# 32 more tokens by gather, score lists at a later rank, gathers from an earlier stage, stored products by fours

## The chip, the cores and the metric

The kernel runs on one core of a Trainium2 chip. The metric is the device time of one execution in microseconds (us). Engines are called TensorE (PE in the rows; PEld is its weight load), VectorE (DVE), ScalarE (ACT), GpSimd (POOL) and SyncE (SP, which here only issues transfers).

## The reference

Two transformer blocks on 512 tokens of width 1024. The part that the change touches is the expert layer of the first block (PEER): 16,384 experts, each a row of `u` and a row of `v`; each token picks, for each of 8 heads, 16 experts by product keys.

```
q = (t @ wq).reshape(128, 8, 2, 128)
s = einsum('tpcd,pckd->tpck', q, sub_keys)
s1, i1 = top_k(s[:, :, 0], 16);  s2, i2 = top_k(s[:, :, 1], 16)
cand = s1[..., :, None] + s2[..., None, :]          # 256 sums
top, pos = top_k(cand, 16);  idx = i1*128 + i2 at pos
g = softmax(top)
a = gelu(einsum('tpkd,td->tpk', u[idx], t))
y = einsum('tpk,tpkd->td', g * a, v[idx])
x = x + gt2 * y
```

## The kernel before

Tokens are in four blocks of 128. For blocks 0 to 2 (`ND = NDENSE = 3`, `nd = 384` tokens) the layer is computed densely: for each of 128 groups `e` of 128 experts, all products with all tokens, times a matrix of gates that is zero for experts not picked. Block 3 is computed by gathers: `gather` (L834) fetches with an indirect transfer from GpSimd, for each of 128 picks, one row of `u` and `v` a token (1 MB), takes the dot product with `h2` (L840), gelu, gate, and adds the weighted `v` row to `pacc` (L846), in pairs of two picks; `run_gather` issues pairs up to a count. The sum of both ways is in f32: each dense product is three fp32r matmuls of a high and a low part (`split`: the cast `wh` on ScalarE, L190, and the difference `wl` on VectorE, L191; `mm` at L176 issues every matmul).

Stages, with their times in the profiled execution:

- 547 to 680 us, query stage (L799 to 812): for j = 0..7 a projection of `h2` by two weight tiles of `wq` (48 matmuls of 512 columns), then scores against the keys into `rsc`, kept for all j. At odd j `gemv_T` (L248) computes one modulation vector: eight weight tiles `wg` (own buffers, two), four small matmuls each, a copy of the row (`row`), eight `pick` matmuls that turn it into a column, and one add into `modT`.
- 680 to 905, U stretch (`s_part`, L681): for each expert group e, 24 matmuls `pS` of 384 columns, gelu into `S`; the first `PRE = 52` groups are stored to HBM (`sd`). VectorE works beside it through `routing` of blocks 3, 2, 1, 0: the lists of the 16 best per score vector (`top16`, five operations), the candidates, and the one-hot comparisons that read out the picks.
- 905 to 1165, one-hot stage: twelve groups of 32 tokens. For each, three more `s_part`, and four batches of 8 tokens: comparisons `Rh` and `Lq` on VectorE, `Lq` times gate (three batches by 8 ScalarE operations each, the fourth by one VectorE pass), 64 `pG` matmuls that make the gate matrix, stored to HBM as `gd`; one pair of gathers.
- 1165 to 1840, V stretch: for each of 128 steps, gate block `Gt` and product block `Sr` (from HBM, or `S` fresh from `s_part` for the 40 groups from `NSP = 88` on) give `W`; `W` is split, and 18 matmuls `po` of 512 columns add it times `v`. The other 104 gathers run beside it.
- From 1840 on: block by block `x`, loaded back from `x1d` (L961), plus the gated sum, a norm chain (`xsq`, `ss`, `rr`, `xs`), eight transposes and a split give the second block's input; then that block's projections start.

All weight tiles pass through a ring of four (`wr`) with rings for `wh` and `wl`. A scheduler orders each engine's instructions by a priority that follows the order in the program, moved by `issue_after`; a pool's buffer comes free when its last reader is done.

Of the kernel before, what the change touches and what calls it, by code (L numbers as in the profile page):

```python
# [10 lines left out]
F32 = mybir.dt.float32  # L11
# [113 lines left out]
NS = 10  # L125
NSP = 88
PRE = 52
GEN = 3
GR = 1
LAST = 4  # L130
# [5 lines left out]
def program(tc, a, out, tap=None):  # L136
# [37 lines left out]

    def mm(ps, lhs, rhs, first=True, last=True):
        PE.matmul(ps, lhs, rhs, start=first, stop=last)  # L176
# [438 lines left out]
    nd = ND * P  # L615
# [8 lines left out]
    gd = dp.tile([32, P, ND * 4, P], F32, name="gd")  # L624
    sd = dp.tile([NSP, P, ND * P], F32, name="sd")
    mp = pool(eM, "mid")
    gt2T = modT[:, 5, :]
    h2g = {b: mp.tile([P, D], F32, name=f"h2_{b}") for b in range(ND, NB)}
    idx = {b: mp.tile([P, P], I32, name=f"idx{b}") for b in range(ND, NB)}
    gate = {b: mp.tile([P, P], F32, name=f"gate{b}") for b in range(ND, NB)}  # L630
# [3 lines left out]
    def h2_of(b, x):  # L634
        t = h2g[b] if b in h2g else st.tile([P, D], F32, name="h2t")
# [62 lines left out]
    for e in range(EARLY):  # L698
        DMA.dma_start(sd[e], s_part(e, V.tensor_tensor))
# [15 lines left out]
    def top16(src, w, val, pos):  # L715
        t = r2.tile([P, P], F32, name="mr", bufs=2)[:, :w]
# [8 lines left out]
    def routing(b, sc):  # L725
        sv = r2.tile([P, 16, 16], F32, name="sv", bufs=2)
        si = r2.tile([P, 16, 16], U32, name="si", bufs=2)
        for j in range(16):
            top16(sc[:, j, :], P, sv[:, j, :], si[:, j, :])
# [39 lines left out]
        for s_ in range(2):  # L769
            eq = r2.tile([P, 8, 16, 16], BF16, name="eq", bufs=2)  # L770
# [496 lines left out]
```

## Time and profile before

| | |
|---|---|
| median of 3 runs | 2345.69 us (2344.76 to 2349.6) |
| profiled execution | 2337.86 us, its span 2336.1 |
| TensorE busy | 2259.9 us (97%) |
| VectorE busy | 1598.4 us (68%) |
| ScalarE busy | 980.3 us (42%) |
| GpSimd busy | 249.1 us (11%) |
| moved by DMA | 481.74 MB, mean 206 GB/s |

Busy time is the union of an engine's instructions; matmuls are pipelined, so the distance between two starts, not the length of one, tells what a matmul costs. The granted clock is the share of full speed that TensorE had. The largest groups on TensorE are the three kinds of `pS` (1024 each) and the three kinds of `po` (768 each).

### The profile page before, as it was taken

How to read it: one execution, taken by the hardware profiler on the slowest of the kernel's cores; microseconds unless marked ns; L12 is line 12 of the kernel's file. 1: busy time of each engine (PE TensorE's matmuls, PEld its weight loads, DVE VectorE, ACT ScalarE, POOL GpSimd, SP SyncE). 2: the span in 40 equal slices, each digit the busy share in tenths (PEclk: the TensorE clock that was granted, in tenths of full speed). 3: DMA queues.
4: the chain of work that ended last, by engine and by line, in shares of the span. 5: the costliest groups of instructions: out<-in, count | busy, mean ns of one | idle time of the engine just before them, and what ended most of it. 6: DMA issues, size and time to landing. Idle time of an engine off the chain costs nothing. (4 is left out here: it accounts for less than half of the span.)

```text
span 2336.1 us, 34601 instructions
## 1 busy us (share of the span) xinstructions
PE 2259.9 (97%) x13097; PEld 1942.3 (83%) x13097; DVE 1598.4 (68%) x3193; ACT 980.3 (42%) x1828; POOL 249.1 (11%) x159
## 2 busy tenths in 40 slices
PE   7999999998999999999999999999999999989998
PEld 4899986597779999999988888888888786666888
DVE  3674723354359977999689888888898627767344
ACT  4432333333234335877534333333333434446421
POOL 0000000000000000322222222222130000000000
PEclk9999999999999999999999999999999999999999
DMA  7111135625555574999999999999997231120221
GB/s 265 55 57 55 52 118 178 212 101 178 165 196 158 163 258 153 328 320 319 333 360 396 406 347 349 354 362 363 360 380 263 88 103 42 50 86 28 98 92 55
DMA packets 170871, 481.74 MB, mean 206 GB/s; under 512 B 14864, under 2 KB 87952, under 8 KB 153168
## 3 DMA queue, kind: packets, MB, share of 16 engines
q1 hardware_dynamic: 152272, 345.31, 42.7%
q0 software_dynamic: 18432, 134.23, 14.7%
q8 instruction: 103, 1.69, 0.3%
q14 instruction: 64, 0.52, 0.1%
HBM read 431.76 MB, written 46.66 MB: 205 GB/s over the span
## 5 line engine op out<-in xcount | busy, mean ns | idle before, releaser
L191 DVE TENSOR_TENSOR wl<-wr,wh 128x1024 fp32r<-128x1024 f32 (+1 forms) x378 | 456.7, 1211 | 362.3 <-ACT wh L190 359.8
L190 ACT CAST wh<-wr 128x1024 fp32r<-128x1024 f32 (+1 forms) x378 | 394.0, 1043 | 440.4 <-PE pm L176 196.1
L176 PE MATMUL pS<-h2h,wh 128*128 128x384 f32 x1024 | 348.2, 340 | 7.3 <-ACT S L695 7.2
L176 PE MATMUL pS<-h2h,wl 128*128 128x384 f32 x1024 | 346.1, 338 | 0.0
L176 PE MATMUL pS<-h2l,wh 128*128 128x384 f32 x1024 | 345.5, 337 | 0.0
L839 POOL DMA_INDIRECT uv<-in_uv_dram,idx x128 | 225.8, 1764 | 1006.9 <-DVE pacc L846 688.8
L176 PE MATMUL po<-wl,Wh 128*128 128x512 f32 x768 | 299.6, 390 | 1.8 <-DVE wl L191 1.8
L176 PE MATMUL po<-wh,Wl 128*128 128x512 f32 x768 | 299.5, 390 | 0.0
L176 PE MATMUL po<-wh,Wh 128*128 128x512 f32 x768 | 298.9, 389 | 0.0
L176 PEld LDWEIGHTS pS<-h2h,wh 128*128 128x128 f32 x1024 | 193.4, 189 | 11.7 <-ACT S L695 8.7
L176 PEld LDWEIGHTS pS<-h2l,wh 128*128 128x128 f32 x1024 | 193.3, 189 | 2.0 <-issue 0.8
L176 PEld LDWEIGHTS pS<-h2h,wl 128*128 128x128 f32 x1024 | 193.2, 189 | 0.0
L190 ACT CAST Wh<-W 128x384 fp32r<-128x384 f32 x128 | 65.7, 513 | 267.8 <-PE po L176 162.1
L176 PE MATMUL pm<-h2h,wh 128*128 128x512 f32 x432 | 173.5, 402 | 0.2 <-ACT cr L1106 0.2
L176 PE MATMUL pm<-h2h,wl 128*128 128x512 f32 x432 | 171.8, 398 | 0.0
L176 PE MATMUL pm<-h2l,wh 128*128 128x512 f32 x432 | 171.8, 398 | 0.0
L176 PEld LDWEIGHTS po<-wl,Wh 128*128 128x128 f32 x768 | 144.1, 188 | 31.9 <-DVE wl L191 2.6
L176 PEld LDWEIGHTS po<-wh,Wl 128*128 128x128 f32 x768 | 144.1, 188 | 30.3 <-DVE Wl L191 0.3
L176 PEld LDWEIGHTS po<-wh,Wh 128*128 128x128 f32 x768 | 144.2, 188 | 29.2
L846 DVE SCALAR_TENSOR_TENSOR pacc<-uv,dts,pacc 128x1024 f32<-128x1024 f32 x128 | 163.9, 1281 | 1.9
L840 DVE SCALAR_TENSOR_TENSOR pscr<-uv,h 128x1024 f32<-128x1024 f32 x128 | 156.1, 1219 | 1.9 <-DMA uv<-in_uv_dram,idx 0.9
L191 DVE TENSOR_TENSOR Wl<-W,Wh 128x384 fp32r<-128x384 f32 x128 | 70.8, 553 | 47.9 <-ACT Wh L190 47.8
(410 smaller groups left out, 4100.6 us busy)
## 6 DMA issues: line engine op xcount, KB each, us to landing
wr<-in_uT_dram SPq DMA_DIRECT2D x128, 512.0 KB, 6.0
wr<-in_uv_dram SPq DMA_DIRECT2D x128, 512.0 KB, 7.7
gd<-stg SPq DMA_DIRECT2D x12, 2048.0 KB, 12.6
Gt<-gd SPq DMA_DIRECT2D x32, 768.0 KB, 8.4
sd<-S SPq DMA_DIRECT2D x88, 192.0 KB, 3.9
Sr<-sd SPq DMA_DIRECT2D x88, 192.0 KB, 6.8
wr<-in_w_in_dram SPq DMA_DIRECT2D x32, 512.0 KB, 3.6
wg<-in_w_mod_dram SPq DMA_DIRECT2D x32, 512.0 KB, 4.3
```

The costliest lines, as they stand in the source:

```text
L176: PE.matmul(ps, lhs, rhs, start=first, stop=last)
L190: (ehi or S.copy)(hi, src)
L191: (elo or V.tensor_tensor)(lo, src, hi.bitcast(F32), op=OP.subtract)
L839: G.indirect_dma_start(out=uv, out_offset=None, in_=a["uv"], in_offset=bass.IndirectOffsetOnAxis(ap=idx[b][:, j:j + 1], axis=0))
L840: V.scalar_tensor_tensor(scr, uv[:, :D], 1.0, h2g[b], op0=OP.mult, op1=OP.mult, accum_out=dts[b][:, j:j + 1])
L846: V.scalar_tensor_tensor(acc[b], tl[j - j0][:, D:], dts[b][:, j:j + 1], acc[b], op0=OP.mult, op1=OP.add)
```

## The change

32 tokens of block 2 (its last, `XG = 32`) leave the dense part: `nd` is 352, `pS` matmuls have 352 columns, there are 11 groups of 32 tokens in the one-hot stage (`NTG`), and `W` stays 384 wide with a GpSimd memset of its last 32 columns at each step. These tokens are gathered as a fifth set: the 128 picks of 32 tokens are laid out as 32 picks for 128 partitions (small transfers of `h2`, `idx` and `gate`), 32 more gathers in all, and two f32 matmuls with `pick` add the four partial sums into `po`. 20 gathers now run before the one-hot stage (`G0 = 10` pairs), 22 in it, 118 in V. The score lists are taken right behind each j's scores, at a priority 4000 later (`LATER`), from four `rsc` buffers; `routing` takes the blocks in the order 3, 0, 1, 2; its transposes are put behind the last matmul of groups 34, 44 and 50. The eq product has its second operand copied by ScalarE first (`sfx`). The fourth batch of `Lq` times gate goes to ScalarE. `S` has 5 buffers, 84 groups are stored, by fours. `gemv_T` works in two halves with one row of 512 and one add each, and in the query stage takes its weights from the shared ring. `pscr` is dropped: the dot product writes over the `u` row.

The diff, cut to its core:

```diff
-NS = 10
-NSP = 88
-PRE = 52
+NS = 5
+NSP = 84
+PRE = 51
+G0 = 10
+LATER = 4000
+G1 = G0 + 11
+BORDER = (3, 0, 1, 2)
+NLIST = 4
+XG = 32
+HOLD = (34, 44, 50)
...
-    def gemv_T(pl, ps_pool, wname, part, v, slot, bias, tag="pm"):
-        row = pl.tile([P, D], F32, name="row", bufs=1)
+    def gemv_T(pl, ps_pool, wname, part, v, slot, bias, tag="pm", share=False):
...
-                    w = pl.tile([P, 4, GW], F32, name="wg", bufs=2)
+                    w = wpool["w"].tile([P, 4, GW], F32, name="wr") if share else pl.tile([P, 4, GW], F32, name="wg", bufs=2)
...
-            S.copy(row[:, h2 * 512:(h2 + 1) * 512], ps)
-        ps = ps_pool.tile([P, 512], F32, name=tag)[:, :2 * KT].rearrange("p (k o) -> p k o", o=2)
-        for kt in range(KT):
-            mm(ps[:, kt, :], row[:, kt * P:(kt + 1) * P], pick[:, v:v + 2])
-        V.tensor_add(modT[:, slot, :], ps[:, :, 0], bias)
+            row = pl.tile([P, 512], F32, name="row", bufs=1)
+            S.copy(row, ps)
+            ps = ps_pool.tile([P, 512], F32, name=tag)[:, :KT].rearrange("p (k o) -> p k o", o=2)
+            for k in range(4):
+                mm(ps[:, k, :], row[:, k * P:(k + 1) * P], pick[:, v:v + 2])
+            V.tensor_add(modT[:, slot, 4 * h2:4 * h2 + 4], ps[:, :, 0], bias[:, 4 * h2:4 * h2 + 4])
...
-    nd = ND * P
+    nd = ND * P - XG
+    NTG = nd // 32
+    XS = P // XG
...
+        if b == XB:
+            for g in range(XS):
+                DMA.dma_start(h2g[b][g * XG:(g + 1) * XG, :], t[r0:P, :])
...
-            V.scalar_tensor_tensor(scr, uv[:, :D], 1.0, h2g[b], op0=OP.mult, op1=OP.mult, accum_out=dts[b][:, j:j + 1])
+            V.scalar_tensor_tensor(uv[:, :D], uv[:, :D], 1.0, h2g[b], op0=OP.mult, op1=OP.mult, accum_out=dts[b][:, j:j + 1])
...
-            V.tensor_tensor(eq, eq, sif[:, :, s_, :][:, :, :, None].to_broadcast([P, 8, 16, 16]), op=OP.mult)
+            sfx = r2.tile([P, 8, 16, 16], BF16, name="sfx", bufs=1)
+            S.copy(sfx, sif[:, :, s_, :][:, :, :, None].to_broadcast([P, 8, 16, 16]))
+            V.tensor_tensor(eq, eq, sfx, op=OP.mult)
...
+        prio = tc.cur_priority
+        tc.cur_priority = prio + LATER
+        for i, sc in lists:
+            for m in range(2):
+                top16(sc[:, m, :], P, svs[i][:, 2 * j + m, :], sis[i][:, 2 * j + m, :])
+        tc.cur_priority = prio
...
-    for b in reversed(range(NB)):
-        routing(b, scs[b])
+    for b in BORDER:
+        routing(b)
+    run_gather(G0)
...
-                    if t8 == 24:
-                        V.tensor_tensor(Lh, Lq, bc(g_), op=OP.mult)
-                    else:
-                        for j in range(8):
+                    for j in range(8):
...
-                Ss[e] = d2.tile([P, nd], F32, name="Sr")
-                DMA.dma_start(Ss[e], sd[e])
+                if e % 4 == 0:
+                    Sr = d2.tile([P, 4, nd], F32, name="Sr")
+                    DMA.dma_start(Sr.rearrange("p a b -> p (a b)"), sd[e // 4].rearrange("p a b -> p (a b)"))
+                Ss[e] = Sr[:, e % 4, :]
...
-            W = d2.tile([P, nd], F32, name="W")
+            W = d2.tile([P, ND * P], F32, name="W")
+            G.memset(W[:, nd:], 0.0)
...
-                run_gather(GR * ND * 4 - (GR * ND * 4 - len(todo)) * (n + 1) // (P - 10))
+                run_gather(G1 + (len(todo) - G1) * (n + 1) // (P - 10))
...
+            if b == XB:
+                for hf in range(2):
+                    mm(po[b, hf][r0:P, :], pick[:, :XG], acc[b][:, hf * 512:(hf + 1) * 512], False, False)
```

What stands in a row on TensorE before, in the query stage inside the projection of step j = 2 (`pm<-h2`), with the small matmuls of the modulation product (`tp<-wg`) of step 1:

```order
L176 MATMUL pm<-h2l,wh 128x512
L176 MATMUL tp<-wg,cvec 32x256 x4
L176 MATMUL pm<-h2h,wl 128x512
L176 MATMUL pm<-h2h,wh 128x512
L176 MATMUL pm<-h2l,wh 128x512
L176 MATMUL pm<-h2h,wl 128x512
L176 MATMUL pm<-h2h,wh 128x512
L176 MATMUL tp<-wg,cvec 32x256 x4
```

The same place now, on TensorE from the key matmuls of an odd step to the projection of the next:

```order
L185 MATMUL pm<-keysT,pqT 128x128 x3
L185 MATMUL tp<-wr,cvec 32x256
L185 MATMUL pm<-keysT,pqT 128x128 x5
L185 MATMUL tp<-wr,cvec 32x256 x14
L185 MATMUL tp<-pick,row 128x2 x4
L185 MATMUL tp<-wr,cvec 32x256 x16
L185 MATMUL tp<-pick,row 128x2 x4
L185 MATMUL pm<-h2h,wh 128x512
L185 MATMUL pm<-h2l,wh 128x512
```

The small matmuls, four at a time between projection matmuls before, are now two blocks with the pick matmuls of each half behind, and the projection follows them all.

VectorE before, around the add into `modT` in the same stage:

```order
L718 MAX_INDEX si<-sv,rsc_4985 128x8
L191 TENSOR_TENSOR wl<-wr,wh 128x1024
L261 TENSOR_TENSOR modT<-tp,vecs 128x8
L191 TENSOR_TENSOR wl<-wr,wh 128x1024
L717 MAX sv<-rsc_4985 128x8 x2
```

VectorE now, at the second half's add of the first pair of steps (the first half's add stands 25 list operations ahead of it):

```order
L773 MATCH_REPLACE mr<-sv_5020,rsc 128x128
L774 MAX sv_5020<-mr 128x8
L775 MAX_INDEX si_5024<-sv_5020,mr 128x8
L270 TENSOR_TENSOR modT<-tp,vecs 128x4
L200 TENSOR_TENSOR wl<-wr,wh 128x1024 x4
L771 MAX sv_5021<-rsc 128x8 x2
L772 MAX_INDEX si_5025<-sv_5021,rsc 128x8
```

The adds now stand between list operations, and the four `wl` of the next two projections stand behind the second.

SyncE's transfers before, at the end of the one-hot stage:

```order
L685 DMA wr<-in_uT_dram 128x1024
L961 DMA x_16847<-x1d 128x1024
L887 DMA gd<-stg 128x32x128
L685 DMA wr<-in_uT_dram 128x1024 x2
L926 DMA Sr<-sd 128x384
```

SyncE's transfers now, at the end of V:

```order
L971 DMA wr<-in_uv_dram 128x1024 x10
L207 DMA wr<-in_w_sb_dram 128x1024
L1039 DMA smask<-in_smask_dram 128x256
L1041 DMA cmask<-in_cmask_dram 128x512
L207 DMA wr<-in_w_sb_dram 128x1024 x5
L1005 DMA x_17075<-x1d 128x1024
L1005 DMA x_17072<-x1d 128x1024
```

Block 3's `x` was loaded ahead of the V stretch; the four loads of `x` now stand behind the last loads of `v` and six weight loads of the second block.

## Rows read from the trace of the kernel before

**Rows 1.** Stretches: start:end us, length, busy us (instructions) by engine, granted clock, DMA share, GB/s.

```profile
668.00:905.00 237.00, 232.71 (x1356) 225.99 (x1355) 195.89 (x838) 86.79 (x121) 5.48 (x4) 0.99 0.57 183
1200.00:1820.00 620.00, 618.20 (x2894) 531.87 (x2893) 541.24 (x746) 228.99 (x355) 146.06 (x96) 1.00 0.93 354
```

**Rows 2.** Timeline of TensorE, 94 to 100 us: start us, us, engine, line, operation.

```profile
94.75 0.39 PE L176 MATMUL pm<-hTh,wh 128*128 128x512 f32 x1
...
98.83 0.28 PE L176 MATMUL pm<-wh,hTh 128*128 128x256 f32 x1
```

**Rows 3.** Timeline of TensorE in the U stretch: first and last of 77 matmuls.

```profile
859.69 0.33 PE L176 MATMUL pS<-h2h,wh 128*128 128x384 f32 x1
...
872.87 0.33 PE L176 MATMUL pS<-h2l,wh 128*128 128x384 f32 x1
```

**Rows 4.** Stretches: one group of the one-hot stage.

```profile
1021.00:1041.00 20.00, 19.98 (x138) 19.66 (x137) 18.42 (x20) 15.95 (x40) 5.62 (x2) 1.00 0.93 317
```

**Rows 5.** Timeline of TensorE in the one-hot stage.

```profile
1033.56 3.73 PE L176 MATMUL pG<-Rh,Lq 128*128 128x128 f32 x32
```

**Rows 6.** Groups by line, 1021 to 1141 us: count, busy us, mean ns, idle before.

```profile
L879 ACT ACTIVATE Lq<-Lq,selT 128x128 f32<-128x128 f32 x144 | 44.1, 391 | 2.0 <-DVE Lq L874 2.0
```

**Rows 7.** Timeline of TensorE in the query stage: small matmuls of a modulation product.

```profile
642.96 1.06 PE L176 MATMUL tp<-wg,cvec 128*32 128x256 f32 x14
...
659.28 1.84 PE L176 MATMUL tp<-pick,row 128*128 128x2 f32 x16
```

**Rows 8.** Waits, 547 to 668 us: who for whom, us in total, times, longest.

```profile
PE tp L176 <- DMA wg<-in_w_ada_dram: 2.0, 4, 0.7
...
PE tp L176 <- DMA wg<-in_w_mod_dram: 1.4, 2, 0.8
```

**Rows 9.** DMA issues, 547 to 668 us: count, KB each, median us to landing.

```profile
wg<-in_w_ada_dram SPq DMA_DIRECT2D x19, 512.0 KB, 4.2
...
wr<-in_wq_dram SPq DMA_DIRECT2D x9, 512.0 KB, 4.7
```

**Rows 10.** Timeline of VectorE in the U stretch: list operations.

```profile
719.98 0.07 DVE L719 MATCH_VALUE_LOAD mr<-sv,rsc 128x8 f32 x1
...
721.41 0.07 DVE L719 MATCH_VALUE_LOAD mr<-sv,rsc 128x8 f32 x1
```

**Rows 11.** Groups by line, 547 to 668 us.

```profile
L190 ACT CAST wh<-wr 128x1024 fp32r<-128x1024 f32 x15 | 15.7, 1048 | 37.6 <-PE pm L176 34.8 <-issue 2.7
...
L257 ACT COPY row<-tp 128x512 f32<-128x512 f32 x6 | 3.5, 588 | 9.2 <-PE tp L176 9.2
```

**Rows 12.** Groups by line of VectorE, 668 to 905 us.

```profile
L772 DVE TENSOR_TENSOR eq<-eq,sif 128x2048 bf16<-128x2048 bf16 x8 | 18.2, 2285 | 0.0
...
L721 DVE FIND_INDEX8 si<-sv,mr 128x8 uint32<-128x128 f32 x52 | 14.6, 283 | 0.0
```

**Rows 13.** Groups by line, 1200 to 1820 us.

```profile
L840 DVE SCALAR_TENSOR_TENSOR pscr<-uv,h 128x1024 f32<-128x1024 f32 x98 | 119.5, 1220 | 1.9 <-DMA uv<-in_uv_dram,idx 0.9
```

**Rows 14.** DMA, 1200 to 1820 us: GB/s in 40 slices of 15.5 us.

```profile
GB/s 396 303 417 403 370 411 416 399 405 272 392 362 369 275 394 392 346 329 323 383 382 291 359 415 374 410 366 312 388 383 363 283 387 400 388 370 371 213 228 137
```

**Rows 15.** Timeline at the end of V, TensorE and VectorE.

```profile
1836.41 1.23 DVE L969 TENSOR_TENSOR x<-x,fin 128x1024 f32<-128x1024 f32 x1
...
1839.67 0.39 PE L176 MATMUL po<-wh,Wl 128*128 128x512 f32 x1
...
1844.30 0.56 PE L176 MATMUL pm<-wh,h2h 128*128 128x256 f32 x1
...
1845.70 0.75 DVE L979 TENSOR_SCALAR xs<-x,rr 128x1024 f32<-128x1024 f32 x1
```

**Rows 16.** One tile: the four loads of x from x1d.

```profile
DMA to landing us min/median/max: 2.6/5.0/12.2
```

**Rows 17.** Stretches after the gap at 1840 us.

```profile
1840.00:1850.00 10.00, 8.28 (x35) 6.43 (x34) 8.72 (x17) 8.51 (x19) 1.85 (x1) 0.68 0.32 107
...
1860.00:1870.00 10.00, 9.19 (x64) 9.00 (x65) 3.52 (x8) 3.95 (x8) 0.00 (x0) 0.83 0.01 2
```

More of the change, by code (lines that the diff above doesn't have):

```diff
@@ L173, in program @@
     DMA.dma_start(vecs, a["vecs"])
+    last_mm = [None]
     def mm(ps, lhs, rhs, first=True, last=True):
-        PE.matmul(ps, lhs, rhs, start=first, stop=last)
+        last_mm[0] = PE.matmul(ps, lhs, rhs, start=first, stop=last)
     class Split:
@@ L698, in program, with gather, run_gather @@
     for e in range(EARLY):
[L699 removed]
+        DMA.dma_start(sd[e // 4, :, e % 4, :], s_part(e, V.tensor_tensor))
+    ug = pool(eM, "uvg", 1)
+    nfB = ug.tile([P, D], F32, name="nfB")
+    DMA.dma_start(nfB, a["rows"][0:1, :].to_broadcast([P, D]))
+    S.activation(nfB, nfB, AF.Square)
+    gt2 = ug.tile([P, D], F32, name="gt2")
+    acc = {b: ug.tile([P, D], F32, name=f"pacc{b}") for b in range(ND, NB)}
+    eU = ExitStack()
+    up = pool(eU, "uv", 4)
+    ux = pool(eU, "uvx", 1)
+    acc[XB] = ux.tile([P, D], F32, name="paccx")
+    dts = {b: ux.tile([P, n], F32, name=f"dts{b}") for b, n in ncol.items()}
+    for b in acc:
+        V.memset(acc[b], 0.0)
+    GRP = 2
+    def gather(b, j0):
+        tl = []
+        for j in range(j0, j0 + GRP):
+            uv = up.tile([P, 2 * D], F32, name="uv")
+            G.indirect_dma_start(out=uv, out_offset=None, in_=a["uv"], in_offset=bass.IndirectOffsetOnAxis(ap=idx[b][:, j:j + 1], axis=0))
+            V.scalar_tensor_tensor(uv[:, :D], uv[:, :D], 1.0, h2g[b], op0=OP.mult, op1=OP.mult, accum_out=dts[b][:, j:j + 1])
+            tl.append(uv)
+        ds_ = dts[b][:, j0:j0 + GRP]
+        S.activation(ds_, ds_, AF.Gelu)
+        V.tensor_mul(ds_, ds_, gate[b][:, j0:j0 + GRP])
+        for j in range(j0, j0 + GRP):
+            V.scalar_tensor_tensor(acc[b], tl[j - j0][:, D:], dts[b][:, j:j + 1], acc[b], op0=OP.mult, op1=OP.add)
+    todo = [(b, j0) for b, n in ncol.items() for j0 in range(0, n, GRP)]
+    prog = [0]
+    def run_gather(upto):
+        for k in range(prog[0], min(upto, len(todo))):
+            gather(*todo[k])
+        prog[0] = max(prog[0], upto)
     eR = ExitStack()
@@ L790, in routing @@
             ps = tp.tile([P, 512], F32, name="tp").rearrange("p (k c) -> p k c", k=4)
-            for j, t in enumerate((sel[0], sel[1], gt_)):
-                PE.transpose(ps[:, j, :], t, ident)
+            with tc.issue_after(after[HOLD[b]].ins):
+                for j, t in enumerate((sel[0], sel[1], gt_)):
+                    PE.transpose(ps[:, j, :], t, ident)
             S.copy(selT[b], ps[:, :3, :])
-    scs = [rb.tile([P, 16, P], F32, name=f"rsc{i}") for i in range(NB)]
     for j in range(8):
@@ L802, in program @@
             S.copy(qT[:, m, :], ps)
-        for i in range(NB):
+        lists = []
+        for i in BORDER:
             ps = pm.tile([P, 512], F32, name="pm")
@@ L814, in program @@
     V.tensor_mul(modT[:, 7, :], modT[:, 7, :], nfT)
+    after = {}
     for e in range(EARLY, PRE):
-        DMA.dma_start(sd[e], s_part(e))
-    for b in reversed(range(NB)):
-        routing(b, scs[b])
-    eR.close()
-    ug = pool(eM, "uvg", 1)
-    nfB = ug.tile([P, D], F32, name="nfB")
-    DMA.dma_start(nfB, a["rows"][0:1, :].to_broadcast([P, D]))
-    S.activation(nfB, nfB, AF.Square)
-    gt2 = ug.tile([P, D], F32, name="gt2")
-    eU = ExitStack()
-    up = pool(eU, "uv", 4)
-    acc = {b: ug.tile([P, D], F32, name=f"pacc{b}") for b in range(ND, NB)}
```

91 lines of the change are left out of this document (42 added, 49 removed).

## Prediction

> **What bounds the kernel now.** I read the table of stretches first. In the U stretch (668 to 905 us) TensorE is busy 232.71 of 237 us, in the V stretch (1200 to 1820) 618.20 of 620, both at a granted clock of 0.99 to 1.00 [rows 1]. So in these two TensorE's own columns are the bound, and columns taken away are time, if nothing else comes last. But the others are close: VectorE 541.24 of 620 in V and 195.89 of 237 in U, the DMA queues a share of 0.93 at 354 GB/s in V [rows 1]. The one-hot stretch is tighter still: in one group of 20 us TensorE 19.98, VectorE 18.42, ScalarE 15.95, DMA 0.93 [rows 4]. Next I read the cadence of the matmuls, then the small stages that the change rewrites: the query stage (547 to 680), and the end of V. The profiled execution took 2337.86 us, which is 7.8 below the median of the timed runs; I add up the change against the profiled execution and move the result to the median at the end.
>
> **Columns taken away.** Eighteen 512-column matmuls start from 94.75 to 98.83: 0.2267 us each [rows 2]. The 76 intervals of 384-column ones from 859.69 to 872.87 give 0.1734 [rows 3]. The difference is 0.0533 for 128 columns, 0.416 ns a column, so 32 columns fewer save 13.3 ns. All 128 expert groups have 24 such matmuls: 3072 x 13.3 ns = **-41.0**. One group of 32 tokens fewer in the one-hot stretch takes 64 pG matmuls away, and 32 of them take 3.73 [rows 5]: **-7.5**. The V matmuls stay 3 x 256 of 512 columns and W is filled up with zeros, so there nothing is saved. Two f32 matmuls of 512 columns that add the 32 tokens into the result are new; nothing here shows that form. Each lies between one pass of 0.2267 and four: 0.5 to 1.8 for both, and I take the upper end, as f32 operands go undivided: **+1.8**.
>
> **The query stage.** Before, the four modulation products (32 small matmuls each) have weight tiles of their own, are spread between projection matmuls, and TensorE lost only 2.0 + 1.4 us to their loads [rows 8]. Now they share the ring of four weight tiles with the projections and stand in one block, in two halves (order of PE, above). Take a pair of query steps, from the end of the second one's key matmuls (time 0). Seven of the small matmuls (14 rows) take 1.06 [rows 7], so the first half's remaining 14 end at 2.1; copy of the row 0.59 [rows 11], four pick matmuls 0.9 (eight, in 16 records, took 1.84 [rows 7]) end at 3.7 (the second half's place in PSUM is then free only after the modT add). The fifth weight tile goes into the ring place that the first freed at about 0.3; it lands 4.2 later [rows 9], at 4.5. The second half runs 4.5 to 6.9, copy and picks end at 8.5. The next projection's weights go into the place that the fifth tile frees at 5.1 and land 4.7 later [rows 9], at 9.8; the cast takes 1.05 [rows 11]; the projection starts at 10.9. Without waits the block would end at 6.3 (32 small matmuls 4.8, picks 1.8, less 0.3 at the start), so 4.6 are lost. On VectorE the modT adds now stand inside the lists: 25 list operations lie between the two halves' adds and four wl passes are behind the second (order of DVE). Six list operations take 1.43 (719.98 to 721.41 [rows 10]), so 25 take 6.0; the second add is done at about 10, before the cast, and wl, 1.2 like other passes of 128x1024 [rows 13], at 12.1; its first user is the third matmul, due at 11.4: 0.6 more. That is 5.2 a pair, 21 for four, less the 3.4 of before: **+17**. It can be 8 if the list work is further ahead than this, since then only the landing times remain, and 35 if the clock falls in each gap (below).
>
> **The U stretch.** Products are the same, shorter by the columns counted above. VectorE loses most list work: 52 lists' second searches are in this stretch [rows 12], at 5 operations of 0.238 a list some 55 with the partly finished ones, of which some 10 may still spill in; the eight eq products get a contiguous operand, and I estimate half of their 2.29 [rows 12] (no row shows it; between all and half): -9. Twenty gathers come in at 2.5 (two passes like the 1.22 of [rows 13], and a read of the sum): +51. So 195.9 - 45 - 9 + 51 = 193 for VectorE, against 48 groups x 24 x 0.160 = 184 on TensorE and some 14 until the first one-hot matmul. A tie, in which the wl that TensorE waits for stand between gathers: **+4**, from 0 (all in the slack) to 15.
>
> **The one-hot stretch.** A group takes 72 x 13.3 ns = 1.0 less on TensorE, 19.1. ScalarE takes over the fourth batch of gate products: 8 more at 0.306 (144 took 44.1 [rows 6]), 15.95 + 2.45 = 18.4. VectorE is relieved by one pass, to 17.2. ScalarE is not the bound, but has 0.7 left instead of 4: **+1**, 0 to 10.
>
> **The V stretch.** Gathers go from 104 to 118 here, fresh groups from 40 to 44, stored ones from 88 to 84. VectorE: 87% of the stretch [rows 1], so about 588 of the 675 from the one-hot stretch's end to the last V matmul; +14 x 2.5 + 4 x 1.2 - 5 for narrower W = 622, against some 677 on TensorE (44 x 3.84 + 522, part of it done before the stretch, as now). 92% busy, and it feeds both TensorE and the gathers' buffers. The 128 memsets of W (GpSimd, 128x32) stand between gathers, which on GpSimd mostly wait for the pacc two gathers back; the multiply that needs one comes at least five VectorE operations after that pacc, so I price them at nothing; if a memset comes late, W, Wh, Wl and the matmuls come late, and that is inside the range. Bytes: 118 MiB gathered, 64 of v, 22 of u, 21 stored blocks of 0.69 MiB and 32 Gt of 0.69 make 252 MB where the same sum was 240. Over 677 us that is 372 GB/s; stretches of 15.5 us had up to 417 [rows 14]. **+5**, 0 to 25.
>
> **The end of V.** Before, block 3's x is loaded before the one-hot stretch ends (order of SP) and its norm chain ends inside V; the last V matmul starts at 1839.67 and the first projection of the next block at 1844.30 [rows 15]. Now the load of x for all blocks stands behind six weight loads, of which the fifth must wait for a ring place that is freed by a wl after the last V matmuls. It lands a median 5.0 after its issue [rows 16], and then the whole chain follows: from the add of x for block 0 at 1836.41 to its xs at 1845.70 it was 9.3 [rows 15], with other blocks between; then eight transposes and the split, which took the 4.4 above. So the first projection starts some 5 + 6 to 9 + 4 = 15 to 18 after V, not 4.6 [rows 15]: 11 to 13 for this one, but the blocks behind it come sooner after it than before, since their po is done while x is awaited: **+10**, 4 to 16. The attention stage's products in halves, one row buffer: **+1**, 0 to 4.
>
> **Sum.** -41.0 - 7.5 + 1.8 + 17 + 4 + 1 + 5 + 10 + 1 = **-8.7**: 2329.2 for a profiled execution, and 2345.69 - 8.7 = **2337** for the median. About 49 us of work go, and some 40 come back as waits in places that were covered.
>
> **Rivals.**
> (B) The new waits are mostly covered: the query stage at its low end (+8), the end of V at +4, the rest nothing: -48.5 + 1.8 + 12 = -34.7, **2311**. For it: TensorE's idle time was only 4.3 in U and 1.8 in V [rows 1], so the old order covered nearly all. Against it: the ring place and the x load are freed by work that ends at that very point.
> (C) V becomes bound by its transfers: if the mean of before, 354 GB/s at a share of 0.93 [rows 1], is what the queues give, 252 MB take 712 us, where I have 677 + 5: +30, sum +21, **2367**, slower. It decides from about 365 GB/s down. Against it speak the slices of 411 to 417 in the same stretch [rows 14]; for it, that slices near 280 stand between them and that gathers land with the loads of v in one queue set.
> The Trainium skill (DMA: Bandwidth & Descriptors, section Specifications) gives about 358 GB/s as what HBM yields per core, which speaks for C: by that figure the stretch would be an estimated 704 us and the sum about +13. The rows of 411 to 417 are above it, so here it is no ceiling over 15.5 us.
> (D) The clock falls in the query stage's gaps. After the gap at 1840 the granted clock was 0.68 from 1840 to 1850 and 0.83 from 1860 to 1870 [rows 17]: 4.9 us lost for one gap of this kind; four of them +20, sum +11, **2357**, slower. It decides if TensorE is idle as long as there; my gaps are 0.8 and 2.4 us, with work between.
> (E) The narrower matmuls are not shorter: +41, **2378**. Cadences on one line for 384 and 512 [rows 2, 3] speak against it.
>
> **Chances and range.** My forecast, with a sum between -22 and +1: 0.46, of which 0.36 is over 0.2% faster (4.7 us, about what a measurement tells from no change) and 0.10 within. B 0.17, faster. C 0.17, slower. D 0.15, of which 0.13 slower and 0.02 within. E 0.05, slower. Together: faster 0.53, within 0.2% 0.12, slower 0.35. Both signs hold much, so the likeliest case's own range is 2324 to 2347; the range for 8 in 10 reaches to B's and C's middle, 2309 to 2366.
>
> **What would show it.** Right: 352-column matmuls 0.160 apart; one-hot groups every 19.1 to 20; four gaps in the query stage of 4 to 6 us together, released by a load of the shared ring or by wh; V at 675 to 690 with TensorE over 97% busy; 15 to 18 us from the last V matmul to the next projection. Wrong: V longer than 700 with VectorE or the DMA share at 1.0 (C); clock under 0.9 in the query stage (D); no gaps there, or x landed before V ends (B).

## The result, and the profile after

The changed kernel is slower: 2370.99 us (median of four runs, 2364.68 to 2375.21) against 2345.23 for the kernel before in the same comparison (four runs, 2337.61 to 2349.6). The ratio is 1.0107, with a 95% interval of 1.0087 to 1.0126. The forecast was 2337, with a range of 2309 to 2366: the sign is wrong, and the time lies 5 us above the range.

The profiled execution of after took 2364.68 us. Section 1 of its page, busy time of each engine, share of the span, instructions:

```profile
span 2362.9 us, 34702 instructions
## 1 busy us (share of the span) xinstructions
PE 2239.3 (95%) x13037; PEld 1910.7 (81%) x13037; DVE 1647.3 (70%) x3295; ACT 1001.3 (42%) x1908; POOL 317.5 (13%) x319
```

TensorE is busy for 20.6 us less than before (2259.9 us), although its clock was lower (a mean granted clock of 0.972 against 0.992). The span is 26.8 longer. So the columns did go; waiting came in their place. I cut both traces at the same events and compare the lengths of the pieces, since spans also differ by where a run's first 530 us end, and a profiled execution can lie well off its kernel's median (2354.72 against 2337.62 in the first experiment). The borders are the first and last `keysT` matmul (query stage), the first and last `pG` (one-hot stage), the first and last `po<-wh,Wh` of the V stretch, and the first matmul that makes the second block's scores (`pS<-bkT,bqT`). All in us, worked out from the first and last starts of these tiles:

| stage | before | after | difference | forecast |
|---|---|---|---|---|
| query | 121.6 | 140.9 | +19.3 | +17 |
| U | 236.9 | 234.6 | -2.3 | -17.4 |
| one-hot | 227.9 | 207.6 | -20.3 | -28.6 |
| last `pG` to first `po` | 41.4 | 23.5 | -17.9 | with V |
| V | 652.9 | 682.8 | +29.9 | -17.9 and +29.9 together: +9.4 |
| last `po` to the second block's scores | 106.0 | 124.4 | +18.4 | +10 |
| from there to the end | 390.9 | 390.8 | -0.1 | +1 |

The forecast column puts the prediction's terms into these stages. Four products move behind the one-hot stage, three from that stage and one from U (U evicts 51 products `S` instead of 52). In U, which as cut here also holds the first one-hot group's three products, 54 products by 0.32 us (24 matmuls of 13.3 ns) and one whole product of 24 x 0.1734 make -21.4, with +4 for stalls -17.4. One one-hot group of 20 and thirty products by 0.32, +1 for ScalarE, make -28.6. In the gap and V, 40 fresh groups by 0.32 less, four more by 3.84, +5 and +1.8 make +9.4.

Where TensorE waits in after (who for whom, us in total, times, longest), in the query stage, in U, at the start of V and at its end:

```profile
PE tp L185 <- ACT row L266: 4.3, 6, 0.8
PE tp L185 <- DMA wr<-in_w_ada_dram: 4.0, 7, 1.1
PE tp L185 <- DVE si L775: 1.5, 1, 1.5
PE tp L185 <- DVE sv L771: 1.2, 1, 1.2
...
PE pS L185 <- ACT S L713: 11.9, 9, 3.7
...
PE po L185 <- ACT Wh L199: 7.9, 1, 7.9
...
PE pS L1029 <- DVE xs L1023: 16.4, 2, 15.8
```

(`row` is the copy of a modulation product, `si` and `sv` are lists on VectorE.) Before, the query stage's largest waits for loads were 2.0 and 1.4 [rows 8]; in U TensorE was idle 4.3 in all [rows 1], and from the last `po` to the next projection it was 4.6 [rows 15]. The stretches around them, with length, busy us (instructions) of PE, PEld, DVE, ACT and POOL, granted clock, DMA share and GB/s:

```profile
547.00:600.00 53.00, 49.58 (x259) 37.37 (x258) 27.17 (x135) 12.27 (x21) 0.00 (x0) 0.87 0.46 151
575.00:580.00 5.00, 2.82 (x38) 1.69 (x28) 4.46 (x30) 0.59 (x1) 0.00 (x0) 0.86 0.75 238
580.00:585.00 5.00, 3.86 (x32) 0.61 (x24) 4.69 (x27) 0.54 (x1) 0.00 (x0) 0.50 0.91 334
585.00:590.00 5.00, 4.90 (x16) 4.18 (x17) 2.89 (x6) 3.15 (x4) 0.00 (x0) 0.50 0.81 297
590.00:595.00 5.00, 5.00 (x19) 3.98 (x18) 2.45 (x2) 1.08 (x2) 0.00 (x0) 0.78 0.95 259
700.00:750.00 50.00, 44.15 (x282) 39.53 (x275) 46.75 (x214) 25.10 (x28) 0.00 (x0) 0.86 0.68 223
850.00:900.00 50.00, 43.21 (x246) 42.34 (x247) 40.69 (x53) 17.55 (x31) 14.68 (x11) 0.93 0.99 377
1210.00:1840.00 630.00, 627.59 (x3029) 542.73 (x3029) 557.98 (x776) 230.82 (x366) 193.50 (x223) 1.00 0.92 360
1250.00:1300.00 50.00, 50.00 (x250) 44.06 (x249) 47.44 (x69) 19.92 (x33) 19.56 (x19) 1.00 1.00 402
1840.00:1900.00 60.00, 38.98 (x202) 30.29 (x201) 31.58 (x56) 25.84 (x51) 5.09 (x4) 0.77 0.23 82
```

Three things are to be read here. V, which had the most rivals, is in order: TensorE busy 627.59 of 630. The clock falls to 0.50 in the query stage from 580 to 590, behind gaps none of which is longer than 1.50 us. And the table's border between query and U cuts the loss in two: the fourth modulation product's block stands behind the last key matmul, from 699.45 on, and only behind it comes the first product of U (TensorE of after):

```profile
704.45 0.72 PE L185 MATMUL tp<-wr,cvec 128*32 128x256 f32 x8 [1.34 <-DVE tv L771]
...
712.33 0.66 PE L185 MATMUL pS<-h2h,wh 128*128 128x352 f32 x1
```

So part of what U lost belongs to the query stage's change.

### The profile page after: what moved, and what is told of

Same layout as the page of the kernel before. It is cut to its first block, busy times and chain, and to the rows that moved or that the text cites. A ratio compares the mean times of both kernels' runs of the same rounds, so it can differ in the third digit from the quotient of the medians.

```text
span 2362.9 us, 34702 instructions
## 1 busy us (share of the span) xinstructions
PE 2239.3 (95%) x13037; PEld 1910.7 (81%) x13037; DVE 1647.3 (70%) x3295; ACT 1001.3 (42%) x1908; POOL 317.5 (13%) x319
## 5 line engine op out<-in xcount | busy, mean ns | idle before, releaser
L737 POOL DMA_INDIRECT uv<-in_uv_dram,idx x160 | 276.1, 1726 | 816.0 <-DVE pacc L744 478.3
L185 PE MATMUL pS<-h2h,wh 128*128 128x352 f32 x1024 | 339.2, 331 | 12.9 <-ACT S L713 12.9
L185 PE MATMUL pS<-h2h,wl 128*128 128x352 f32 x1024 | 336.7, 329 | 3.3 <-DVE wl L200 3.3
L185 PE MATMUL pS<-h2l,wh 128*128 128x352 f32 x1024 | 335.9, 328 | 0.0
L738 DVE SCALAR_TENSOR_TENSOR uv<-uv,h 128x1024 f32<-128x1024 f32 x160 | 193.1, 1220 | 30.3 <-DMA uv<-in_uv_dram,idx 30.2
L185 PEld LDWEIGHTS pS<-h2h,wh 128*128 128x128 f32 x1024 | 195.3, 191 | 17.6 <-ACT S L713 15.8
L741 ACT ACTIVATE dts<-dts 128x2 f32<-128x2 f32 x80 | 16.3, 204 | 224.4 <-DVE uv L738 224.4
L917 ACT ACTIVATE Lq<-Lq,selT 128x128 f32<-128x128 f32 x352 | 109.3, 394 | 4.6 <-DVE Lq L915 4.6
```

Source lines behind the costliest of these rows:

```text
L185: last_mm[0] = PE.matmul(ps, lhs, rhs, start=first, stop=last)
L737: G.indirect_dma_start(out=uv, out_offset=None, in_=a["uv"], in_offset=bass.IndirectOffsetOnAxis(ap=idx[b][:, j:j + 1], axis=0))
L738: V.scalar_tensor_tensor(uv[:, :D], uv[:, :D], 1.0, h2g[b], op0=OP.mult, op1=OP.mult, accum_out=dts[b][:, j:j + 1])
L741: S.activation(ds_, ds_, AF.Gelu)
L917: S.activation(Lh[:, j, :], Lq[:, j, :], AF.Copy, scale=g_[:, tg * 32 + t8 + j:tg * 32 + t8 + j + 1])
```

## The experiments

Times are device us with the ratio to the kernel before and its 95% interval; "stage" means the table's borders. The theory at the start: four separate covers were lost (query weights, ScalarE's order in U, products behind the last `pG`, an early load of x), while the columns are gained as forecast. The rival theory: V pays, by its transfers or VectorE.

### Weights of the modulation products in idle gather buffers

The gathers' buffers `uv` are not used in the query stage, so the weights can go there and leave the ring to the projections:

```diff
-w = wpool["w"].tile([P, 4, GW], F32, name="wr") if share else ...
+w = share.tile([P, 2 * D], F32, name="uv")[:, :D].rearrange("p (k n) -> p k n", k=4) if share else ...
-            gemv_T(rb, tp, "w_mod", 5, 0, 5, bmT[:, 40:48], "tp", True)
+            gemv_T(rb, tp, "w_mod", 5, 0, 5, bmT[:, 40:48], "tp", up)
```

> The changed kernel with one edit: the weights of the modulation products in the query stage go into the four gather buffers, which are idle until the first gather, and not into the ring of the projections' weights. Theory (the shared ring stretches the query stage: small matmuls in a block, loads that start only when places come free, TensorE's clock at half behind the gaps): the last key matmul comes at 680 to 684 us of the profile where it came at 699.2, and the whole is 15 to 20 us shorter, about 2352. Rival (the list operations between the modT adds on VectorE hold the one PSUM place): the gaps released by VectorE stay, the last key matmul comes no earlier than 692, and the whole is at most 8 shorter.

Measured: 2337.62, ratio 0.9951 (0.9929 to 0.9972), more than the 15 to 20 us expected. The query stage is 119.8, 21.1 shorter than in after, and U is 228.4, 6.2 shorter, since the fourth block stands there. The waits of TensorE from 547 to 700 in this kernel, and behind them its stretch from 547 to 600:

```profile
PE tp L185 <- DMA uv<-in_w_ada_dram: 4.0, 3, 1.8
PE tp L185 <- DMA uv<-in_w_mod_dram: 0.5, 2, 0.4
```

```profile
547.00:600.00 53.00, 52.46 (x311) 42.35 (x311) 31.77 (x144) 18.30 (x28) 0.00 (x0) 1.00 0.60 204
```

As much time is still waited for loads (4.5), but the waits for `row`, `si` and `sv` are gone and the clock stays at 1.00. So the shared ring was the cause of the whole +19.3 and of some 6 us of U. It had put the small matmuls into one block; now they stand between projections again. Of the 21.1, 6.9 are fewer waits (11.4 from 547 to 700 in after, 4.5 here). The rest goes along with the clock: 0.87 from 547 to 600 and 0.90 from 600 to 700 in after, 1.00, 1.00 (to 650) and 0.97 here. This one edit alone makes the changed kernel faster than before.

### Lists at the same rank as before, on top of three repairs

The kernel with three repairs is described below (the last experiments); here it has one number changed.

```diff
-LATER = 4000
+LATER = 0
```

> The kernel with the three edits and LATER = 0: the score lists at the priority of their place, ahead of the splits of the next products. Theory (the later rank keeps list operations from delaying wl, and the query stage has VectorE time to spare): the query stage gets 5 to 15 us longer by waits for wl, the rest is the same. Rival (the rank doesn't matter, since VectorE is only half busy there): query stage within 2 us, the whole within 5 of 2325.

Measured: 2329.82, ratio 0.9907 (0.9877 to 0.9938); with 4000 it was 2325.05. The query stage is the same (119.8 against 119.6), U is 233.2 against 224.8. So the rank does not matter in the query stage; in U the later rank is worth 8 us in these two traces (from 700 to 934, TensorE waits 18.6 for `S` without it, 12.3 with it). The whole is 4.8 apart, and the two intervals overlap.

### No gathers before the one-hot stage

```diff
-G0 = 10
+G0 = 0
```

> The changed kernel with one edit: no gathers before the one-hot stage (G0 = 0), so 22 in it and 138 in V. Theory (in the U stretch, gelu of the gathers' dot products waits on ScalarE for VectorE and for transfers, the eviction S stands behind it, and TensorE waits for S): the waits of pS for S in the U stretch fall from 11.9 us to under 4, and the stretch is about 8 shorter; V gets 20 more gathers, 51 us of VectorE, 95% busy, and grows by 5 to 25; the whole between 2365 and 2390. Rival (the list work and the eq products, not the gathers, make S late): waits for S stay over 8.

Measured: 2401.89, ratio 1.0229 (1.0174 to 1.0285). U is 222.0, 12.6 shorter, and V 736.9, 54.1 longer, where 5 to 25 were expected. TensorE's waits in U, and in V from 1210 to 1840:

```profile
PE pS L185 <- ACT S L713: 3.9, 5, 1.1
...
PE po L185 <- DVE wl L200: 15.0, 20, 1.8
PE pS L185 <- DVE wl L200: 12.1, 7, 2.5
PE po L185 <- DVE Wl L200: 6.1, 4, 3.1
```

So the gathers cause U's stall: 11.9 of waits for `S` become 3.9 (in five). The 20 gathers cost V 54.1 / 20 = 2.7 each, about the length of their two VectorE passes and the read (1.28 + 1.22 + 0.08). V with the 118 gathers of the change stands just short of the point where a further gather costs its whole length. VectorE alone is not the bound there: it is busy 566.69 of the 630 us and waits 49.6 for gathered rows (16.4 in after); what the passes and what the transfers cost, no run separates. The chain in U is in the rows of after's ScalarE:

```profile
838.88 0.20 ACT L741 ACTIVATE dts<-dts 128x2 f32<-128x2 f32 x1 [5.59 <-DVE uv L738]
838.99 1.03 ACT L199 CAST wh<-wr 128x1024 fp32r<-128x1024 f32 x1
839.92 0.45 ACT L713 ACTIVATE S<-pS 128x352 f32<-128x352 f32 x1
...
848.84 1.90 ACT L827 COPY sfx<-sif 128x2048 bf16<-128x2048 bf16 x1 [7.16 <-DVE eq L828]
850.65 1.04 ACT L199 CAST wh<-wr 128x1024 fp32r<-128x1024 f32 x1
```

ScalarE's operations run one after another in these rows. A gelu of 0.20 us on two columns (`dts`) waits 5.59 us for a dot product, which waits for its gathered rows (`DVE uv <- DMA uv`, 12.3 us in nine waits) or stands behind other passes; the cast `wh` of the next products and the eviction `S` of the last ones stand behind it, and TensorE runs out of PSUM buffers. The copy `sfx` does the same once, with 7.16, and TensorE then idles 3.72. The run took the gathers away whole, with their VectorE passes and transfers; that the gelu's place in the order is what hurts is read from the rows, not tested alone.

### The copy `sfx` undone

```diff
-            sfx = r2.tile([P, 8, 16, 16], BF16, name="sfx", bufs=1)
-            S.copy(sfx, sif[:, :, s_, :][:, :, :, None].to_broadcast([P, 8, 16, 16]))
-            V.tensor_tensor(eq, eq, sfx, op=OP.mult)
+            V.tensor_tensor(eq, eq, sif[:, :, s_, :][:, :, :, None].to_broadcast([P, 8, 16, 16]), op=OP.mult)
```

> The changed kernel with one edit: no copy sfx on ScalarE, the eq product on VectorE takes its second operand with a stride as before. Theory (most of TensorE's wait for S in the U stretch, 11.9 us, is gelu of gathers that stands ahead of S on ScalarE while it waits for VectorE's dot product; a copy sfx is behind one gap of 3.7 us): the waits for S fall by about 4, and VectorE has 9 us more work, so that the stretch is between 5 shorter and 5 longer. Rival (ScalarE's copies are the cause of all): waits for S fall below 4 and the stretch is 10 shorter.

Measured: 2364.61, ratio 1.0074 (1.0053 to 1.0094). U is not better: 238.2, with 14.1 us of TensorE's waits for `S`, where some 8 were expected. But the one-hot stage is 200.3, 7.3 shorter. The starts of the groups there (from the copies of `pG`) are mostly 19.1 to 19.3 apart in both kernels; in after one is 26.3, which this kernel doesn't have. All nine kernels with 352 columns and the copy have one of 25.3 to 27.0, the three without the copy have none; the kernel with 384 columns (below) has the copy and none. In after, TensorE and ScalarE in it:

```profile
978.81 1.04 ACT L199 CAST wh<-wr 128x1024 fp32r<-128x1024 f32 x1 [4.87 <-DMA wr<-in_uT_dram]
...
980.69 0.79 PE L185 MATMUL pG<-Rh,Lq 128*128 128x128 f32 x2 [4.81 <-ACT Lq L917]
```

It is the chain of U again with another head: a cast waits 4.87 for its weights, and the gate products stand behind it. With the copy, ScalarE has 15.2 us more to do in U and VectorE 8.6 less (the eight products take 1.21 instead of 2.29 [rows 12], as estimated). Why the late load falls away without the copy, the traces don't show.

### Two of the last products kept back to cover the start of V

```diff
+                if 4 * b + tg == NTG - 1:
+                    g_last = last_mm[0]
+                    for e in es_:
+                        DMA.dma_start(sd[e // 4, :, e % 4, :], s_part(e, hold=None if e == es_[0] else g_last))
```

> The changed kernel with one edit: two of the three expert groups of the last one-hot group are issued behind its last pG matmul, so that seven groups (27 us) and not four (15 us) stand between it and the first V matmul. Theory (five kept products are too few to cover the store of the last gate matrix and its load, 22 us from the store's issue to W): the gap of 7.9 us before the first V matmul is gone, the whole is 6 to 9 shorter, about 2363. Rival (the gate load is late because the transfer queues are full at that point, share 0.94): the gap stays, no change.

Measured: 2378.31, ratio 1.0129 (1.002 to 1.0238). The two runs (2368.97 and 2387.64) are too far apart to tell from after by the whole; from the first `pG` to the last `po` the trace is 7.4 longer. The gap at the first `po` is gone, but the products are now missing between the `pG`. TensorE's waits from 1100 to 1210:

```profile
PE pG L185 <- ACT Lq L923: 5.0, 4, 1.9
PE pS L185 <- ACT S L717: 2.7, 1, 2.7
```

So here the work for a cover could not be taken from a group whose other engines need it as theirs.

### The last store of `gd` in two parts

```diff
+                parts = ((0, 8), (8, 32)) if 4 * b + tg == NTG - 1 else ((0, 32),)
+                for q0, q1 in parts:
+                    DMA.dma_start(gd[q0:q1, :, b * 4 + tg, :]...)
```

> The changed kernel with one edit: the store of the last one-hot group's gate matrix is in two transfers, the quarter that the first V steps read ahead of the rest. Theory (the gap of 7.9 us before V is the landing of the 2 MB store and then of the gate load, behind too few kept products): the first gate load can start some 10 us earlier, the gap is under 2 us, the stretch from the last pG to the first po matmul is 16 to 18 us where it was 23.5, the whole 6 to 9 shorter. Rival (the load waits for the whole of the stored array, or the queues are full): gap unchanged.

Measured: 2369.47, ratio 1.0097 (1.0068 to 1.0127). The wait for the first `Wh` is 8.6 against 7.9: nothing gained. The first quarter landed 3.4 us after its issue, but the load of `Sr` that stands ahead of it is issued only when the whole of `stg` has been read, since it is laid over the same memory. After's SyncE rows show the same order:

```profile
1142.32 0.38 SPq L925 DMA_DIRECT2D gd<-stg  x1
1157.52 0.33 SPq L965 DMA_DIRECT2D Sr<-sd  x1
1157.89 0.43 SPq L969 DMA_DIRECT2D Gt<-gd  x1
```

### V's first buffers laid over other memory

The pools of the one-hot stage change places, and V's tiles are laid out in the order of first use, so that the first `Sr` and `Gt` don't lie over `stg` (on top of the three repairs):

```diff
-        gg = pool(es, "ggen", 2)
         oh = pool(es, "oneh", 2)
+        gg = pool(es, "ggen", 2)
...
+        for i in range(LAST):
+            for name, shape, dt, n in (("Sr", [P, 4, nd], F32, 2), ("Gt", [P, NTG, 4, 32], F32, 2), ...
```

> The kernel with the three edits (2325 us), and the buffers of the V stretch laid out so that the first step's tiles (Sr, Gt, W, Wh, Wl) do not lie over the stage buffer stg of the last one-hot group. The split store had not moved the gap before V (7.6 us). Theory (the first Sr and Gt loads wait until the whole last store has read stg, since they overwrite it; the store lands 14.6 after its issue): the first Sr load is issued about 10 us earlier, the gap falls under 2, from the last pG to the first po 15 to 17 us instead of 23.2, the whole 2315 to 2319. Rival (the load waits for the stored array itself, as a whole): gap unchanged, 2325.

Measured: 2326.24, ratio 0.99 (0.9872 to 0.9929), as without it (2325.05). SyncE and VectorE of this kernel at the start of V:

```profile
1115.32 1.00 SPq L929 DMA_DIRECT2D gd<-stg  x2
1122.55 1.32 SPq L983 DMA_DIRECT2D Sr__11117<-sd  x1
1123.97 2.55 SPq L987 DMA_DIRECT2D Gt__11119<-gd  x1
...
1137.14 0.53 DVE L996 TENSOR_TENSOR W__11127<-Sr__11117,Gt__11119 128x352 f32<-128x352 f32 x1 [8.71 <-DMA Gt__11119<-gd]
```

The load of `Gt` is now issued 8.7 us behind the store instead of 15.6 (1157.89 less 1142.32 above), but the multiply that waits for it starts 13.2 later instead of 5.9. From the store to the multiply it is 21.8 us against 21.4, and TensorE's gap is 8.3: the memory under `stg` set when the load was issued, not when it landed. The transfers are full while the load is on its way (a stretch of this kernel, DMA share and GB/s at the end):

```profile
1130.00:1137.50 7.50, 0.05 (x1) 0.00 (x0) 0.36 (x1) 1.41 (x2) 0.12 (x1) 0.63 1.02 423
```

That fits the rival of the two experiments before, full queues, better than a wait for the stored array; a test of it alone is missing.

### Eight `S` buffers instead of five

Without `sfx` there is memory for them (on top of the three repairs, with the old layout):

```diff
-NS = 5
+NS = 8
```

> The kernel with the three edits, without the copy sfx (eq product on VectorE as before), and with the 4 KB that this frees used for eight S buffers instead of five. Theory (the gap before V is a matter of cover: store and load of the gate matrix take 22 us at full queues, and four products behind the last pG last 15; seven last 27): no wait of po for Wh at V's start, from the last pG to the first po 27 to 28 us with three products less in V, so that one-hot end to last po is 7 to 10 shorter than with five buffers, and the whole 2313 to 2318. Rival (the S buffers don't matter, the queues only get later): the gap stays over 5 and the whole is 2323 as with the layout and no sfx.

Measured: 2320.9, ratio 0.989 (0.9864 to 0.9916); neither the theory's 2313 to 2318 nor the rival's lasting gap. The wait for `Wh` is gone: three more products stand behind the last `pG`; 2.2 us came back as a wait for `S`. But from first `pG` to last `po` it takes 912.5 us, where the best kernel with five buffers (the last one below, also without `sfx`) takes about 911.4. The time went into the matmuls: TensorE from 1299.7 on in this kernel and then in after, start, us and operation, the first and last of twelve `po`:

```profile
1299.66 0.40 PE L185 MATMUL po<-wh,Wh 128*128 128x512 f32 x1
...
1302.23 0.39 PE L185 MATMUL po<-wh,Wl 128*128 128x512 f32 x1
```

```profile
1299.70 0.39 PE L185 MATMUL po<-wh,Wl 128*128 128x512 f32 x1
...
1302.19 0.39 PE L185 MATMUL po<-wl,Wh 128*128 128x512 f32 x1
```

That is 2.57 / 11 = 0.234 against 2.49 / 11 = 0.226 apart. At eight places in V the means are 0.2328 to 0.2335 in this kernel and 0.2266 to 0.2280 in after, both at a granted clock of 1.00. 2304 matmuls by 0.0065 make 15 us, more than the gap gave. This is one traced execution, the longest of the six (2325.18). The 352-column matmuls show nothing of it (0.161 in both). What slows them stays open; in this trace it is there over the whole of V, and TensorE is busy all of the 600 us from 1210 on.

### x of block 0 in memory of its own

```diff
-        xt = [xp.tile([P, D], F32, name=f"x{b}") for b in range(NB)]
+        xt = [None] + [xp.tile([P, D], F32, name=f"x{b}") for b in range(1, NB)]
+        xt[0] = pool(top, "xz", side="right").tile([P, D], F32, name="x0")
```

> The changed kernel with one edit: block 0's x tile gets a memory pool of its own, so that the tiles of blocks 1 to 3 do not lie over the split W tiles and can be loaded before V ends. Theory (the loads of x stand behind weight loads that wait for the last V matmuls): block 3's chain ends inside V, the first transpose comes under 2 us after the last V matmul where it came 16 after it, and the whole is 8 to 14 us shorter (block 0's x is still late), about 2358. Rival (the chain itself, ten operations on three engines, is what takes the time behind V): at most 3 shorter.

Measured: 2362.51, ratio 1.0073 (1.0045 to 1.0101). From the last `po` to the second block's scores it takes 113.0, 11.4 shorter. The tiles in the shared pool move with it: three loads of x are now issued from 1134.67 to 1177.55 and only one at 1851.16, and TensorE's largest wait for `xs` falls from 15.8 to 2.4. So the late load of x was the cause, and what made it late was the memory: x lay over buffers that V's last steps still read. With all four early (below) the whole +18.4 is gone.

### The three repairs together, and what the 32 tokens are worth then

One kernel has the weights in `uv`, the split store and room for all four x: `selT` and `ior`, which nothing reads in V, get memory that is given back before it.

```diff
-    selT = [mp.tile([P, 3, P], F32, name=f"selT{b}") for b in range(ND)]
-    ior = mp.tile([P, P], F32, name="ior")
...
+    selT = [selp.tile([P, 3, P], F32, name=f"selT{b}") for b in range(ND)]
+    ior = selp.tile([P, P], F32, name="ior")
...
+    eSel.close()
```

> The changed kernel with three edits: modulation weights in the idle gather buffers, the store of the last gate matrix in two transfers, and selT and ior in memory that is given back before V, so that no x tile lies over the split W and all four can be loaded early. Theory (four separate places, three of them mended): query stage 120 us from first to last key matmul, the gap before V under 2, and from the last V matmul to the first bkT matmul about 106 as in the kernel before; the whole 2370 - 21 - 6 - 8 - 18 = about 2320, faster than both kernels. Rival (they share a bound, VectorE or the transfers, so that mending one place moves the wait to the next): 2340 or more.

Measured: 2325.05 (2318.79 to 2327.3), ratio 0.99 (0.9873 to 0.9928). The gap before V is not mended (23.2 from the last `pG` to the first `po`, 23.5 in after). The query stage is 119.6 and the end of V 105.6, both at or under before's 121.6 and 106.0. V is 689.1, 6 longer than after's: TensorE is idle 5.9 of the 600 us from 1210 on, mostly for `wl`.

The same kernel without the 32 tokens (384 columns, twelve groups, 128 gathers, and the counts that follow from these):

```diff
-XG = 32
+XG = 0
```

> The same three edits on the changed kernel with no tokens of block 2 gathered (XG = 0: 384 columns, 12 one-hot groups, 128 gathers, no memsets; 48 groups before the one-hot stage). Theory (the 32 tokens take 41 + 8 us of columns from TensorE, and the V stretch is just short of bound by VectorE): 30 to 45 us slower than the kernel with the three edits alone. Rival (the gathers cost as much as they save, since VectorE or the transfers bound the U and V stretches): within 10 us of it.

Measured: 2354.59, ratio 1.0027 (1.0016 to 1.0039). So the 32 tokens alone are worth 29.5 us when the covers are there. By stages, read from this kernel's longest execution (2368.26) and so summing to 33.7: one-hot 24.0, U 5.3, the gap 1.9, the end 2.1, V only 1.5, the query stage -1.1. V has 39 x 0.32 = 12.5 us of shorter matmuls and returns nearly all of it: VectorE is busy 530.70 of the 600 us from 1210 on with the tokens, 477.78 without, and TensorE, idle 5.9 with them, is not idle at all without.

The best with five `S` buffers has `sfx` undone as well and the layout above:

> The kernel with the layout of the V stretch, and the copy sfx taken back (eq product on VectorE with a strided operand). Theory (in the kernel as changed this made the one-hot stretch 7 shorter, as ScalarE's casts come sooner after the U stretch, and the U stretch 4 longer): 3 shorter than with the layout alone. Rival (with the gaps before it mended, VectorE is the bound of the U stretch): 5 to 9 longer.

Measured: 2323.32 (2312.84 to 2328.78), ratio 0.988 (0.9841 to 0.992). U is 230.0 and the one-hot stage 200.9, against 227.2 and 206.7 with the layout alone: their sum is 3.0 shorter, as expected. This kernel and the one with eight `S` buffers can't be told apart. Both beat the kernel before by 1.1 to 1.2% and the changed one by some 2%.

## Why the prediction was wrong, step by step

The sum failed in five terms of similar size: the query stage, U's gathers, one group of the one-hot stage, the products behind the last `pG`, and the end of V.

**Columns: right.** The 352-column matmuls are 0.160 to 0.161 apart, most one-hot groups 19.1 to 19.3 (forecast 19.1, before 20.05 by the same copies). The rival E falls.

**Query stage: too small, mechanism half wrong.** The +19.3 against +17 looks right by luck of the border: it holds three of the four blocks, and with the fourth (6.2 of U) it is 25.5, so 8 are missing. The prediction let the next projection's weights land late (at 9.8 of its clock); they did not: they were issued at 580.66 and TensorE went on at 586.83, right behind the picks. What cost instead was rival D's clock, which the prediction allowed only for gaps as long as the one at 1840 [rows 17]. It went to 0.86 and then to 0.50 at gaps of 0.69, 1.50, 0.18, 0.18 and 0.76 us. A rival that decides "if TensorE is idle as long as there" had its point in the wrong place. Start, us, operation and the idle time ahead of it, TensorE of after:

```profile
576.98 1.05 PE L185 MATMUL tp<-pick,row 128*128 128x2 f32 x8 [0.69 <-ACT row L266]
579.53 2.28 PE L185 MATMUL tp<-wr,cvec 128*32 128x256 f32 x16 [1.50 <-DVE si L775]
581.99 1.08 PE L185 MATMUL tp<-wr,cvec 128*32 128x256 f32 x8 [0.18 <-DMA wr<-in_w_mod_dram]
583.26 1.08 PE L185 MATMUL tp<-wr,cvec 128*32 128x256 f32 x8 [0.18 <-DMA wr<-in_w_mod_dram]
585.10 1.86 PE L185 MATMUL tp<-pick,row 128*128 128x2 f32 x8 [0.76 <-ACT row L266]
```

**U: 9 us missed, the wrong engine added up.** Without the fourth block U is 8.5 shorter than before, not 17.4. VectorE's sum (193 busy, measured 204.58) and the `wl` between gathers gave +4; TensorE waited for `wl` once, 1.8, and 11.9 for `S`, and the 20 gathers cost 12.6 where +4 stood. A gather also puts one small gelu into ScalarE's order, ahead of casts and evictions, and that one waits for a dot product and its gathered rows. The prediction counted the gather's VectorE passes and not the order in which its smallest instruction stands. The clock went down with the gaps here, too (0.93 from 850 to 900).

**One-hot: 8 us missed.** The group length is right; one group of 26.3 is 7 of it. The term "+1, 0 to 10" had that in its bounds, but by luck: it is not that ScalarE "has 0.7 left instead of 4", but one cast whose weights land late, in kernels with the copy `sfx`. That copy the prediction priced only as VectorE's relief, and its 15.2 us on ScalarE at nothing.

**Start of V: not in the sum, 7.9 us.** Before, with ten `S` buffers, nine products were made behind the last `pG` (41.4 us), while `gd` was stored and loaded. With five buffers four stand there (4 x 3.84 = 15.4, then 7.89 of waiting). The prediction moved the groups by columns and did not ask what they covered. In after, the multiply on VectorE and the first `po`:

```profile
1163.76 0.96 DVE L978 TENSOR_TENSOR W<-Sr,Gt 128x352 f32<-128x352 f32 x2 [8.33 <-DMA Gt<-gd]
1164.93 0.80 PE L185 MATMUL po<-wh,Wh 128*128 128x512 f32 x1 [7.89 <-ACT Wh L199]
```

**V: right, without its +5.** Less the gap, gap and V together are +4.1 where columns, picks and the +5 made +9.4. The transfers went at 360 GB/s with a share of 0.92 over 630 us, and at 402 in the stretch quoted above, so rival C falls. By the Trainium skill (DMA: Bandwidth & Descriptors, Specifications: about 358 GB/s) C would have decided; the trace disagrees, 402 GB/s over 50 us. Memsets cost nothing, as priced. What the prediction did not see is how little room is left: 20 gathers more there cost 2.7 each.

**End of V: order right, size 18.4 instead of 10.** The fifth weight load stands ahead of x as described (SyncE, TensorE of after). Why x stands there is the memory that it lies over, as the two experiments show: before, all four loads were issued from 1145.2 to 1177.2.

```profile
1824.65 23.88 SPq L207 DMA_DIRECT2D wr<-in_w_sb_dram  x5
1848.58 2.57 SPq L1005 DMA_DIRECT2D x<-x1d  x4
...
1864.32 0.69 PE L1029 MATMUL pS<-ident,xs 128*128 128x128 f32 x2 [15.78 <-DVE xs L1023]
```

The wait of 15.8 lies in the forecast 15 to 18. The mis-sized part is "the blocks behind it come sooner": they did not. Behind the last `po` TensorE is idle 21.0 of 124 us where it was 4.7 of 106; the rest of the 18.4 goes with a clock of 0.77 from 1840 to 1900.

**The sum.** Query 8.5, U 9, one-hot 8, the gap and V 3 net, its end 8, the rest -1: 35.6 of the 35.5 us between -8.7 and +26.8. The prediction said that "the old order covered nearly all" and took it for a sign, in rival B, that the new waits would be covered, too; it priced only the covers that it saw in the diff and the order.

## What to carry to other kernels

When an edit takes buffers or memory away (S from ten to five, x laid over V's split buffers, weights into a shared ring), list what each of them covered and price that cover by the wait that ends last behind it; here three such covers, 25.5 us (ring), 7.9 and 18.4, came to more than the 46.7 of columns saved. Count a new instruction by its place in its engine's order and by what it waits for, not by its own length alone: a gelu of 0.20 us that waited 5.59 had casts and evictions behind it. Don't gather small matmuls with waits between them into one block where they can stand between large ones: here the clock fell to 0.50 in the block and stayed at 1.00 with the same matmuls spread out.

## What the runs showed of the hardware

The granted clock fell to 0.50 (1.2 GHz of 2.4) behind gaps of at most 1.50 us while TensorE ran the small products of 32 columns, and stood at 0.50 until 590 and at 0.78 to 595, although TensorE was busy 4.90 of 5 us from 585 on. With the same products spread out and 4.5 us of waits in all it stayed at 1.00 to 650 us. And matmuls of the same shape at a granted clock of 1.00 were 0.2267 apart in one program and 0.2333 in another, over the whole of a stage; no run here shows why.
